# A Hymba-style layer on one core: the scheduler's simulated-timeline mode, and the down-weight sums moved beside the last short convolutions and the o heads

## The chip, the core and the metric

The kernel runs on one core of one Trainium2 chip. The metric is the device time of one execution in microseconds (us). Five engines take part, each with its own instruction stream that it executes in order: TensorE (PE, with its weight loads shown apart as PEld), VectorE (DVE), ScalarE (ACT), GpSimd (POOL) and SyncE (SP). All transfers between HBM and the on-chip memory are issued from SP's stream, so their issue is in order too: a transfer whose buffer is not free holds up every transfer behind it. An engine that waits for a semaphore holds up its own stream in the same way.

## What is computed

The reference is one layer on 2176 tokens of width 1024: 128 context tokens and 2048 latent tokens that read them. Cut to what matters:

```python
shift1, scale1, gate1, shift2, scale2, gate2 = jnp.split(mod, 6, axis=-1)
h = rmsnorm(x, norm1) * (1 + scale1) + shift1
z = h @ w_in                       # short-conv inputs, q, k, v, o, gates
y_sc = sc_b * conv3(sc_c * sc_x)   # short convolution
h_m = mlstm_bidir(q, k, v, gates, C0, n0, m0)   # forward and backward scans, 4 heads, chunks of 128
x = x + gate1 * (concat([y_sc, norm(h_m) * sigmoid(o)]) @ w_out)
h2 = rmsnorm(x, norm2) * (1 + scale2) + shift2
up = conv3(h2 @ w_up)              # 2 x 2816 columns, conv over a 64-wide grid
x = x + gate2 * ((silu(gg) * a) @ w_down)
```

`mod` comes from the conditioning vectors: `silu(c) @ w_mod + b_mod`, a vector of 6 x 1024 for each of two kinds of tokens. The outputs are the new x and the final context states of the scans.

## The kernel before

**Tiles.** The 2176 tokens lie in six blocks (`BL`): five of 384 columns and one of 256. `BA` are the blocks 0 to 2, `BB` the blocks 3 to 5. Every product in float32 is made from three matmuls of a rounded high part and a low rest: weight high by input high, weight high by input low, weight low by input high (`gemm`, L206 to L208; for v and gates L352 to L354, with the tokens as the stationary operand). `load_w` (L110 to L115) loads a weight slab into `wst` (2 buffers), ACT makes its high part `wh` (L112), POOL its low part `wl` (L115).

**Stages, in order of time.** (1) The modulation vectors of the first norm: 16 loads of 512 KB of `w_mod` (`mod_pe`, L485, tile `wm` with 5 buffers) with 8 PE matmuls each (L488); DVE adds the bias (L490), and the input blocks are normalised (`apply`, L178 to L188: `xt`, `hH`, `hL`). (2) v and gates of block 3, 4, 5 (`vg`), then k heads, q heads and short convolutions of these blocks (`heads`, `shortconv`, results stored in `kD`, `qD`, `yD`). (3) o heads of the same blocks, weight by weight of a block (`by_block`), while h of the blocks 0 to 2 is made (`make_h`, with loads `xt<-in_x` L148, and PE's column transposes L140). (4) v and gates of blocks 0 to 2. (5) The gate phase (`gate_phase`, L640 on, with transposes on PE at L665), woven with the k heads of blocks 0 to 2. (6) The scans (`Mix`, L834 to L881), woven with the rest of the heads and short convolutions of blocks 0 to 2. (7) The output projection (`w_out`, L426 to L470, results stored in `xD`), with the second norm's statistics (L129, L132, L133, L237, L239) and the sums that a Strassen-like scheme needs of the normed input (`sums`, L244 to L265: `F<-xD` loads, DVE sums, stores to `tD`). (8) The up projection (`w_up`, loads `st` L287, parts L295/L296, products L1045 to L1047): two halves of the tokens (`hf`), 22 rows of weight tiles `j` in each, seven products `i` in each row. The seven inputs ("slots") of a half are loaded from `tD` (L275) and split by ACT (L280, `tH`) and DVE (L281, `tL`); the convolution over the grid follows on ACT and DVE (L988 to L1010), and `sums(1)`, the sums for the second half, goes beside the first rows. (9) The down projection (`w_down`, L1199 to L1201), again with seven products, of sums of the weights.

**The sums of the down weights.** `down_sums` (L558 to L584) makes those last sums ahead of time. It works in 8 steps of a load of four pieces of 352 KB (`xs<-in_w_down`, L566), four DVE sums (L576 to L580) and four stores (`wsD<-xs`, L583). `pin` (`tc.keep_in_program_order`) keeps the loads and the DVE sums in the order of the source. The tile `xs` has four buffers and lies in the pool `start`, whose memory the pool `gt` of the gate phase takes over.

**What sets the order.** The source is a set of generators: `run(g, side, every)` takes a step of `g` and then one of `side`. The order written down in this way is a priority, not the order of execution: the tile framework's scheduler orders the instructions of each engine afterwards, subject to data dependencies, buffer counts and `pin`. In the program before it does that in its default mode (`tile.TileContext(nc)`, L1296).

Of the kernel before, what the change touches and what calls it, by code (L numbers as in the profile page):

```python
# [12 lines left out]
AF = mybir.ActivationFunctionType  # L13
# [25 lines left out]
BA = (0, 1, 2)  # L39
BB = (3, 4, 5)  # L40
# [17 lines left out]
def hymba_kernel(ctx: ExitStack, tc: tile.TileContext, I, O):  # L58
# [42 lines left out]
    def run(g, side=None, every=1):  # L101
        for i, _ in enumerate(g):
            if side and i % every == 0:
                next(side, None)
# [90 lines left out]
    def make_h(b, src, norm):  # L195
        return apply(b, load_x(b, src, xp, "xt", 2), norm)
# [120 lines left out]
    with ExitStack() as ph1:  # L317
# [52 lines left out]
        def heads(blocks, hs, w0, dst, func, scale, by_block=False):  # L370
            if by_block:
                ws = [load_w(I["w_in"][w0 + h]) for h in range(H)]
                for b in blocks:
                    for h in range(H):
                        head(ws[h], b, h, hs, dst, func, scale)
                        yield
                return
            for h in range(H):
                w = load_w(I["w_in"][w0 + h])
                for b in blocks:  # L380
                    head(w, b, h, hs, dst, func, scale)
                    yield
# [99 lines left out]
        with tc.tile_pool(name="start", bufs=1, side="right") as stp:  # L482
# [41 lines left out]
            def mod_dve():  # L524
                for mt in range(16, 48):
                    st = stp.tile([P, 1024], F32, name="wm", bufs=5)
                    Q.dma_start(st, I["w_modr"][mt - 16])
                    t = stp.tile([P, 2], F32, name="mt", bufs=2)
                    for v in range(2):
                        jk = pm.tile([P, 2, 512], F32, name="y")  # L530
                        V.scalar_tensor_tensor(jk.rearrange("p a b -> p (a b)"), st, 1.0, cB[:, v], op0=ALU.mult, op1=ALU.mult,
                                               accum_out=t[:, v:v + 1])
                    V.tensor_scalar(modT[:, mt, :], t, bmod[:, mt:mt + 1], None, op0=ALU.add)
                    if mt == 39:
                        affine(1, 0, KT)
                    yield
# [10 lines left out]
            def first_stats():  # L547
                for b in BA:
                    ss = squares(b, load_x(b, I["x"], xp, "xt", 2))
                    yield  # L550
                    inv_rms(ss, BL[b][1], rcol(b))
                    yield
# [31 lines left out]
                    t = nt  # L584

            late()
            side = chain(first_stats(), mod_dve())
            run(vg((3,), hs, ws), prep(4))
            run(vg((4,), hs, ws), prep(5))
            run(vg((5,), hs, ws))  # L590
            run(heads(BB, hs, 16, kD, AF.Copy, 1.0), side, 2)
            run(heads(BB, hs, 12, qD, AF.Copy, QS), side, 2)
            run(shortconv(BB, hs), side)
            run(side)
            go = heads(BB, hs, 20, oD, AF.Sigmoid, 1.0, by_block=True)
            dsums = down_sums()
            for b in BA:
                run(islice(go, 4), dsums)
                hs[b] = make_h(b, I["x"], 0)
            run(vg(BA, hs, load_vg(0) + load_vg(1)), dsums)  # L600
            run(dsums)

        ml = phr.enter_context(tc.tile_pool(name="ml", bufs=1, side="right"))

# [296 lines left out]
                    next(fill, None)  # L901


        with tc.tile_pool(name="gt", bufs=1, side="right") as gt:
            gph = gate_phase()
            kh = heads(BA, hs, 16, kD, AF.Copy, 1.0)
            while True:
                try:
                    next(gph)
                except StopIteration as e:  # L910
                    cols, colc, decB = e.value
                    break
                next(kh, None)
                next(kh, None)
            run(kh)
# [392 lines left out]
```

## Time and profile before

| | |
|---|---|
| Median of 3 runs | 2552.67 us (2550.52 to 2553.85) |
| The profiled execution's own time | 2555.34 us |
| Its span in the trace | 2553.5 us |
| PE busy | 2470.7 us of the span, 16127 matmuls |
| DVE, ACT, POOL busy | 1649.2, 1112.7, 566.4 us |
| Bytes moved | 444.60 MB, mean 174 GB/s |

So 1.84 us lie around the span, and the profiled execution is 2.67 us above the median of the runs. Busy time of PE includes the time in which its granted clock is low, so a stage can be short of work and show few idle microseconds: the rows by stage show busy time and granted clock (PEclk, 1.00 is full speed) side by side, then the DMA share and the GB/s moved. A chain-of-waits row is a start, a duration and the work or transfer that the following step waited for.

### The profile page before, as it was taken

The page shows a single profiled execution, that of the slowest core. Times are in us where ns is not written, and L with a number is a line of the kernel's source. Part 1 is how long each engine was busy: PE and PEld are TensorE (multiplying, and loading weights), DVE is VectorE, ACT ScalarE, POOL GpSimd, SP SyncE. Part 2 cuts the span into 40 slices and gives each one's busy share as a digit, 9 for nine tenths or more (in the row PEclk, how much of TensorE's full clock was granted, in tenths as well). Part 3 has the DMA queues.
Part 4 walks back from the last instruction along what each step waited for, and adds up shares of the span by engine and source line. Part 5 has one row for each costly group of instructions (what it writes and reads, how often), then busy time and mean ns, then how long its engine had stood idle before and what let it go on. Part 6 is the DMA issues. An engine that isn't in the chain of part 4 may idle for free.

```text
span 2553.5 us, 42533 instructions
## 1 busy us (share of the span) xinstructions
PE 2470.7 (97%) x16127; PEld 2366.4 (93%) x16127; DVE 1649.2 (65%) x2741; ACT 1112.7 (44%) x2035; POOL 566.4 (22%) x470
## 2 busy tenths in 40 slices
PE   8999998999999889899999999899999999999998
PEld 8999997999999889899999999788888899999998
DVE  3993255222356666678678666877776796687586
ACT  4522142222245554455455444555554554444342
POOL 2442142211233443422112111122122100000000
PEclk9999998999999999999999999999999999999999
DMA  7771188356567887775125222522222277767674
GB/s 280 252 270 69 66 278 284 117 168 178 180 191 241 253 261 226 251 270 173 67 81 181 83 83 82 171 92 99 83 91 93 72 227 227 242 214 225 187 218 135
DMA packets 281423, 444.60 MB, mean 174 GB/s; under 512 B 23282, under 2 KB 206722, under 8 KB 279554
## 3 DMA queue, kind: packets, MB, share of 16 engines
q1 hardware_dynamic: 281218, 441.88, 53.0%
q8 instruction: 127, 2.08, 0.3%
q14 instruction: 78, 0.64, 0.1%
HBM read 335.31 MB, written 106.48 MB: 173 GB/s over the span
## 4 chain that ended last, share of the span: by engine, by line
PE 77%; DMA 8%; DVE 7%; issue 3%; ACT 3%; POOL 2%; SPq 1%; DVEq 0%; ACTq 0%; POOLq 0%
PE acc L206 8%; PE acc L208 8%; PE acc L207 8%; PE pa L1045 7%; PE pa L1047 7%; PE pa L1046 6%; PE d L1200 5%; PE d L1201 5%; PE d L1199 5%; PE pb L1045 3%; PE pb L1046 3%; PE pb L1047 3%; PE pc L1045 2%; PE pc L1046 2%; PE pc L1047 2%
## 5 line engine op out<-in xcount | busy, mean ns | idle before, releaser
L206 PE MATMUL acc<-hH,wh 128*128 128x384 f32 (+1 forms) x1536 | 515.4, 336 | 8.2 <-DVE row L462 5.5
L208 PE MATMUL acc<-hH,wl 128*128 128x384 f32 (+1 forms) x1536 | 508.0, 331 | 0.5 <-POOL wl L115 0.5
L207 PE MATMUL acc<-hL,wh 128*128 128x384 f32 (+1 forms) x1536 | 507.8, 331 | 0.0
L1199 PE MATMUL d<-bh,wh 128*128 128x272 f32 x1232 | 355.7, 289 | 0.7 <-ACT raw L1057 0.7
L1201 PE MATMUL d<-bh,wl 128*128 128x272 f32 x1232 | 356.1, 289 | 0.0
L1200 PE MATMUL d<-bl,wh 128*128 128x272 f32 x1232 | 355.4, 289 | 0.0
L1045 PE MATMUL pa<-tH,wh 128*128 128x288 f32 (+1 forms) x1056 | 347.7, 329 | 3.7 <-DVE raw L1059 2.0
L1047 PE MATMUL pa<-tH,wl 128*128 128x288 f32 (+1 forms) x1056 | 346.9, 329 | 1.0 <-DVE wl L296 1.0
L1046 PE MATMUL pa<-tL,wh 128*128 128x288 f32 (+1 forms) x1056 | 346.9, 329 | 0.0
L296 POOL TENSOR_TENSOR wl<-st,wh 128x512 fp32r<-128x512 f32 x132 | 184.2, 1396 | 696.2 <-ACT wh L295 668.4
L115 POOL TENSOR_TENSOR wl<-wst,wh 128x512 fp32r<-128x512 f32 (+1 forms) x160 | 235.2, 1491 | 441.8 <-ACT wh L112 417.5
L206 PEld LDWEIGHTS acc<-hH,wh 128*128 128x128 f32 x1536 | 292.9, 191 | 10.2 <-DVE row L462 5.1
L208 PEld LDWEIGHTS acc<-hH,wl 128*128 128x128 f32 x1536 | 292.6, 190 | 1.2 <-POOL wl L115 1.0
L207 PEld LDWEIGHTS acc<-hL,wh 128*128 128x128 f32 x1536 | 293.1, 191 | 0.3 <-issue 0.2
L988 DVE SCALAR_TENSOR_TENSOR tt<-raw,fw,tt 128x127 f32<-128x127 f32 (+4 forms) x264 | 246.1, 953 | 2.7 <-ACT tt L994 1.5
L1199 PEld LDWEIGHTS d<-bh,wh 128*128 128x128 f32 x1232 | 231.9, 188 | 1.3 <-ACT raw L1057 1.1
L1200 PEld LDWEIGHTS d<-bl,wh 128*128 128x128 f32 x1232 | 231.9, 188 | 0.2
L1201 PEld LDWEIGHTS d<-bh,wl 128*128 128x128 f32 x1232 | 231.8, 188 | 0.0
L1045 PEld LDWEIGHTS pa<-tH,wh 128*128 128x128 f32 x1056 | 198.4, 188 | 20.2 <-ACT c L1052 2.2
L1047 PEld LDWEIGHTS pa<-tH,wl 128*128 128x128 f32 x1056 | 199.1, 189 | 17.0 <-DVE wl L296 1.4
L1046 PEld LDWEIGHTS pa<-tL,wh 128*128 128x128 f32 x1056 | 198.7, 188 | 15.7
L295 ACT ACTIVATE wh<-s 128x512 fp32r<-128x512 f32 x176 | 110.9, 630 | 177.7 <-PE pc L1046 92.0
(239 smaller groups left out, 4848.6 us busy)
## 6 DMA issues: line engine op xcount, KB each, us to landing
st<-in_w_up SPq DMA_DIRECT2D x88, 512.0 KB, 4.3
us<-uD SPq DMA_DIRECT2D x48, 544.0 KB, 5.0
wst<-in_w_in SPq DMA_DIRECT2D x48, 512.0 KB, 4.0
uD<-tt SPq DMA_DIRECT2D x44, 544.0 KB, 2.7
R<-nD SPq DMA_DIRECT2D x34, 512.0 KB, 4.2
wm<-in_w_modr SPq DMA_DIRECT2D x32, 512.0 KB, 5.2
wst<-in_w_out SPq DMA_DIRECT2D x24, 512.0 KB, 4.7
st<-wsD SPq DMA_DIRECT2D x32, 384.0 KB, 3.3
```

The source lines that it names most:

```text
L115: G.tensor_sub(wl[:, a:a + n // 2], st[:, a:a + n // 2], wh[:, a:a + n // 2].bitcast(F32))
L206: PE.matmul(acc[:, :n], w_h, hH[:, k, :n], start=(k == 0), stop=False)
L207: PE.matmul(acc[:, :n], w_h, hL[:, k, :n], start=False, stop=False)
L208: PE.matmul(acc[:, :n], w_l, hH[:, k, :n], start=False, stop=(k == KT - 1))
L296: (G if on_pool else V).tensor_sub(wl, a, wh.bitcast(F32))
L988: V.scalar_tensor_tensor(o, i, w, o, op0=ALU.mult, op1=ALU.add)
L1045: PE.matmul(acc, wh[:, w], rh, start=(kk == 0 and i in (0, 1, 5)), stop=False, skip_group_check=True)
L1046: PE.matmul(acc, wh[:, w], rl, start=False, stop=False, skip_group_check=True)
L1047: PE.matmul(acc, wl[:, w], rh, start=False, stop=(kk == 3), skip_group_check=True)
L1199: PE.matmul(acc, wh[:, c], uh, start=(kk == 0), stop=False)
L1200: PE.matmul(acc, wh[:, c], ul, start=False, stop=False)
L1201: PE.matmul(acc, wl[:, c], uh, start=False, stop=(kk == KH - 1))
```

## The change

Three edits. First, the scheduler is asked for its mode `schedule_with_timeline_sim=True`, in which it orders the instructions against another simulated timeline; every instruction of the program may take another place on its engine. Second, `down_sums()` is appended to `side`, which is taken along in the k heads, q heads and short convolutions of the blocks 3 to 5 and now in the o heads too; what is left of it is run after the o heads. Third, `vg(BA, ...)` is taken out of the pool `start` and run without side work, just before the pool `gt`.

```diff
@@ -584,21 +584,18 @@
             late()
-            side = chain(first_stats(), mod_dve())
+            side = chain(first_stats(), mod_dve(), down_sums())
             run(vg((3,), hs, ws), prep(4))
             run(vg((4,), hs, ws), prep(5))
             run(vg((5,), hs, ws))
             run(heads(BB, hs, 16, kD, AF.Copy, 1.0), side, 2)
             run(heads(BB, hs, 12, qD, AF.Copy, QS), side, 2)
             run(shortconv(BB, hs), side)
+            go = heads(BB, hs, 20, oD, AF.Sigmoid, 1.0, by_block=True)
+            for b in BA:
+                run(islice(go, 4), side)
+                hs[b] = make_h(b, I["x"], 0)
             run(side)
-            go = heads(BB, hs, 20, oD, AF.Sigmoid, 1.0, by_block=True)
-            dsums = down_sums()
-            for b in BA:
-                run(islice(go, 4), dsums)
-                hs[b] = make_h(b, I["x"], 0)
-            run(vg(BA, hs, load_vg(0) + load_vg(1)), dsums)
-            run(dsums)
@@ -901,6 +898,7 @@
+        run(vg(BA, hs, load_vg(0) + load_vg(1)))
         with tc.tile_pool(name="gt", bufs=1, side="right") as gt:
@@ -1293,7 +1291,7 @@
-    with tile.TileContext(nc) as tc:
+    with tile.TileContext(nc, schedule_with_timeline_sim=True) as tc:
```

Line numbers up to 584 stay; those of the gate phase and the scans fall by 3 (L665 becomes L662), those behind L899 by 2 (L1045 becomes L1043).

How the instructions move is seen at three places. The **first** is SP's stream between the o heads and the gate phase. `vD<-rv` stores v of a chunk, `wsD<-xs` a sum of down weights, `wst<-in_w_in` loads the first k weights of the gate phase. Before:

```order
L566 DMA xs<-in_w_down 128x704 x4
L358 DMA vD<-rv 128x258
L583 DMA wsD<-xs 128x704 x4
L358 DMA vD<-rv 128x258 x3
L583 DMA wsD<-xs 128x704 x4
L358 DMA vD<-rv 128x258 x4
L110 DMA wst<-in_w_in 128x1024
L668 DMA sm_4511<-in_state_m 1x8
```

Now:

```order
L566 DMA xs<-in_w_down 128x704 x2
L148 DMA xt<-in_x 128x4x384
L110 DMA wst<-in_w_vg 128x1056
L358 DMA vD<-rv 128x258
L110 DMA wst<-in_w_in 128x1024
L358 DMA vD<-rv 128x258 x2
L583 DMA wsD<-xs 128x704 x2
L110 DMA wst<-in_w_in 128x1024
L583 DMA wsD<-xs 128x704
L358 DMA vD<-rv 128x258
L583 DMA wsD<-xs 128x704
L358 DMA vD<-rv 128x258 x3
```

Before, the last sums are stored behind 14 of the 18 stores of v of the blocks 0 to 2, and the first k weights are loaded behind all of them; now the last sum is stored behind four of them, and both loads of k weights stand ahead of that store. The first load of down weights moves too: from behind the last short convolution's last store (`yD<-yr`) to behind that of the last but one. On PE the first transposes of the gate phase (`S`, from `fc` and `ic`) stood between the last v product and the first k product. Before:

```order
L354 MATMUL acc_4388<-wh_3817,hL_3765 128x264
L665 MATMUL S_4505<-ident_78,fc_4426 128x128
L665 MATMUL S_4508<-ident_78,ic_4425 128x128
L206 MATMUL acc_4447<-hH_3396,wh_4442 128x384
L207 MATMUL acc_4447<-hL_3397,wh_4442 128x384
```

Now the products of two k heads' blocks (`acc_4447` and `acc_4475`, 24 matmuls each) stand ahead of the first transpose, and the third's ahead of the second:

```order
L206 MATMUL acc_4475<-hH_3642,wh_4442 128x384
L207 MATMUL acc_4475<-hL_3643,wh_4442 128x384
L208 MATMUL acc_4475<-hH_3642,wl_4444 128x384
L662 MATMUL S_4505<-ident_78,fc_4426 128x128
L206 MATMUL acc_4527<-hH_3808,wh_4442 128x384
```

The **second** place is SP's stream at the start, from the third load of `w_mod` on (`wm<-in_w_mod`; `cB` are the conditioning vectors of both kinds, `xs` and `xt` input blocks). Before, up to the last of the 16:

```order
L485 DMA wm<-in_w_mod 128x1024 x2
L148 DMA xt<-in_x 128x4x384 x2
L485 DMA wm<-in_w_mod 128x1024 x4
L110 DMA wst<-in_w_vg 128x1056 x2
L485 DMA wm<-in_w_mod 128x1024 x8
```

Now, from the eighth of them on, up to the last and the first load behind it:

```order
L485 DMA wm<-in_w_mod 128x1024
L148 DMA xs<-in_x 128x4x256 x2
L485 DMA wm<-in_w_mod 128x1024 x2
L110 DMA wst<-in_w_vg 128x1056
L485 DMA wm<-in_w_mod 128x1024
L110 DMA wst<-in_w_vg 128x1056
L485 DMA wm<-in_w_mod 128x1024 x2
L148 DMA xt<-in_x 128x4x384
L485 DMA wm<-in_w_mod 128x1024 x2
L110 DMA wst<-in_w_in 128x1024
L485 DMA wm<-in_w_mod 128x1024
L527 DMA wm<-in_w_modr 128x1024
```

The inputs of block 5 (`xs`), the second pair of `w_vg` slabs, one input piece of block 0 (`xt`) and one k weight have moved ahead of the last loads of `w_mod`; in the rows just above these the 1 MB of `cB`, the masks and convolution weights and the inputs of block 4 (two loads of 768 KB) have moved ahead of the eighth.

The **third** place is SP's stream where the up projection begins. `F<-tD_72` loads a slot of the first half, `xD<-row` stores the output projection, `tD_73<-F` stores sums for the second half, `eD` and `uD` are stores of the first rows. Before:

```order
L464 DMA xD<-row 128x384
L275 DMA F<-tD_72 128x1152
L464 DMA xD<-row 128x256
L287 DMA st<-in_w_up 128x1024
L439 DMA row<-in_x 128x384
```

Now:

```order
L464 DMA xD<-row 128x256
L275 DMA F<-tD_72 128x1152
L275 DMA F<-tD_72 128x2304 x4
L999 DMA eD<-raw_11462 128x128
L287 DMA st<-in_w_up 128x1024
L275 DMA F<-tD_72 128x2304
L287 DMA st<-in_w_up 128x1024
L999 DMA eD<-raw_11463 128x128
L244 DMA F<-xD 128x2x256 x4
L265 DMA tD_73<-F 128x7x256 x2
L1008 DMA uD<-tt 128x1088
```

Before, five stores of `xD` stand behind the first slot's load, and the next two slots' loads stand between them; now all slots' loads stand behind the last store of `xD`. The stores of `tD_73` have moved forward as well: before, four of the eight stand at this place and the other four behind the weights of six further rows `j`; now all eight stand here, the last behind the weights of three further rows.

## The prediction

> **What bounds the kernel now.** I read the page first, then busy time and granted clock by stretch, then the waits of PE and the chain of waits in the stretches that fall short. The page:
>
> ```profile
> PE 2470.7 (97%) x16127; PEld 2366.4 (93%) x16127; DVE 1649.2 (65%) x2741; ACT 1112.7 (44%) x2035; POOL 566.4 (22%) x470
> ...
> PE 77%; DMA 8%; DVE 7%; issue 3%; ACT 3%; POOL 2%; SPq 1%; DVEq 0%; ACTq 0%; POOLq 0%
> ```
>
> PE is the bound: it is busy in all but 82.8 us of the span (2553.5 less 2470.7), and the change neither adds nor takes away a matmul, a transfer or a sum. So all that it can win or lose is time in which PE waits or runs at a low clock, and the question is at which places the new order lets it wait. Where PE is steady there is nothing to win; the first fence below shows stretches at full clock beside the one place where the old order was worst, the gate phase (columns: stretch and its length, PE busy with matmuls, PEld, DVE, ACT, POOL, granted clock, DMA share, GB/s):
>
> ```profile
> 320.00:384.00 64.00, 61.59 (x426) 61.20 (x424) 37.20 (x60) 29.53 (x62) 28.39 (x25) 1.00 0.81 281
> 384.00:400.00 16.00, 10.19 (x65) 9.92 (x66) 12.96 (x19) 6.03 (x12) 7.77 (x9) 0.79 0.79 272
> 400.00:432.00 32.00, 32.00 (x267) 32.00 (x266) 12.22 (x23) 3.98 (x12) 0.89 (x9) 1.00 0.92 318
> 432.00:448.00 16.00, 10.17 (x43) 8.86 (x42) 8.63 (x30) 6.00 (x9) 5.42 (x6) 0.68 0.70 228
> 448.00:512.00 64.00, 63.24 (x348) 60.60 (x348) 16.68 (x52) 18.24 (x37) 15.19 (x12) 0.95 0.34 115
> ```
>
> PE has two holes of 5.8 us each, and the clock falls with them. Its waits there (engine, tile, line, what it waited for, us in all, times, longest) and the chain of waits:
>
> ```profile
> PE acc L352 <- ACT xt L186: 5.2, 1, 5.2
> PE S L665 <- DVE fc L658: 4.9, 1, 4.9
> PE acc L353 <- POOL rv L356: 1.6, 1, 1.6
> PE st L140 <- DVE xt L178: 1.4, 1, 1.4
> ```
>
> ```profile
> 399.61 7.05 DMA wsD<-xs
> ...
> 410.94 7.74 DMA wsD<-xs
> ...
> 422.00 8.12 DMA wsD<-xs
> 430.19 5.38 DMA wsD<-xs
> ...
> 439.33 0.49 PE S L665
> ```
>
> The stores of the down weights' sums lead from 399.6 to 435.6, and the gate phase, whose tiles take over the memory of `xs`, can begin only behind the last of them. The transposes and the first k weights, which stand behind all stores of v in SP's stream, come late for that reason. The other hole, at 384 to 400, is the making of h of block 0, on DVE behind the sums.
>
> **Part 1, the sums and the gate phase.** In the new order the first load of down weights stands one short convolution earlier, the last store behind four instead of fourteen stores of v, and the first k weights ahead of it; the gate transposes stand behind two and three finished k products. So the 5.2 and the 4.9 should go: 10.1 us. The clock that the holes cost is, by the rows, 0.21 of 10.19, 0.32 of 10.17 and 0.05 of 63.24: 2.1 + 3.3 + 3.2 = 8.6 us. Together 18.7. The 1.6 and the 1.4 are chains on ACT, DVE and POOL that no row of the new order shortens for certain; I leave them in. Term: -18, with bounds of -23 (idle 2.4 + 5.8 + 5.8 + 0.8 = 14.8, and 8.6) and -8 (the waits go only in part, below).
>
> [...]
>
> **Part 2, the start.** The sixteenth load of `w_mod` gates the last slice (k = 7) of h of block 3 and with it the end of every v product.
>
> ```profile
> 0.00:10.00 10.00, 4.30 (x20) 4.33 (x21) 0.56 (x4) 1.50 (x2) 0.40 (x8) 1.00 0.70 246
> 10.00:20.00 10.00, 8.99 (x78) 8.83 (x78) 4.52 (x11) 3.96 (x8) 0.00 (x0) 1.00 1.04 404
> 20.00:30.00 10.00, 8.34 (x76) 8.26 (x75) 4.30 (x15) 4.49 (x7) 6.10 (x6) 1.00 0.80 316
> 30.00:40.00 10.00, 10.00 (x92) 10.00 (x92) 6.31 (x17) 3.83 (x7) 3.20 (x3) 1.00 0.85 278
> 48.00:56.00 8.00, 8.00 (x56) 8.00 (x55) 1.38 (x5) 3.89 (x8) 0.10 (x1) 0.79 0.89 282
> ```
>
> ```profile
> PE acc L354 <- POOL hL L188: 2.7, 1, 2.7
> ```
>
> ```profile
> 51.44 0.22 PE acc L352
> ```
>
> Before, 16 loads of 0.52 MB, two slabs of 0.54 and two input pieces of 0.79, with the small ones 11.2 MB, stand up to and with it. At the mean of the first four rows (311 GB/s) that is 36 us. Now two more slabs, `cB` (1.05), four `xs` (2.6), one `xt`, one k weight and the masks stand ahead of it: 17.5 MB, 56 us at 311 GB/s and 43 at the 404 of the second row, so 7 to 20 us later. Against that, PE has more v products ahead of the first that needs k = 7 (53 matmuls against 23): 30 of them at half of the 0.22 of the chain's row (its stretch has the clock 0.79) are 3.3 us, and the wait of 2.7 us for POOL, which was splitting slabs, is covered. So +1 to +14; in the middle +7, of which I take off 1, since the loads pulled ahead needn't be waited for later. Term: +6, bounds 0 and +14. [...]
>
> **Part 3, scans and output projection.** The largest wait is one inside the scans:
>
> ```profile
> PE y L851 <- DVE R L838: 14.9, 7, 4.4
> ```
>
> PE's order is nearly the old one there; the weights of the output projection and the input rows are loaded earlier, some matmuls follow their DVE inputs more closely. I take -3, bounds -8 (half of the 14.9 goes) and +5 (a third more of it).
>
> **Part 4, where the up projection begins.**
>
> ```profile
> 1060.00:1090.00 30.00, 24.55 (x147) 24.02 (x146) 23.49 (x42) 14.39 (x28) 10.70 (x9) 0.87 0.89 288
> 1090.00:1120.00 30.00, 29.15 (x193) 28.88 (x192) 21.61 (x36) 12.37 (x20) 5.57 (x5) 0.96 0.83 274
> 1120.00:1150.00 30.00, 27.54 (x194) 26.97 (x193) 21.80 (x27) 19.18 (x31) 6.92 (x5) 0.94 0.72 256
> 1150.00:1200.00 50.00, 49.54 (x372) 49.33 (x371) 48.44 (x74) 29.09 (x50) 12.97 (x10) 1.00 0.54 176
> 1200.00:1400.00 200.00, 200.00 (x1503) 199.79 (x1501) 144.49 (x226) 98.97 (x171) 41.30 (x31) 1.00 0.34 116
> ```
>
> ```profile
> PE acc L206 <- DVE row L462: 4.1, 2, 3.3
> PE st L129 <- DVE rc L132: 2.8, 1, 2.8
> PE pc L1045 <- ACT tH L280: 2.5, 2, 2.2
> PE st L237 <- ACT rb L239: 2.2, 1, 2.2
> ```
>
> ```profile
> 1128.85 8.30 DMA F<-tD
> ...
> 1138.24 1.16 ACT tH L280
> ```
>
> ```profile
> L250 DVE SCALAR_TENSOR_TENSOR F<-F,ab,rb 128x512 f32<-128x512 f32 x16 | 12.6, 804 | 0.9 <-DMA F<-xD 0.9
> ...
> L257 DVE TENSOR_TENSOR F<-F 128x256 f32<-128x256 f32 x8 | 8.6, 1069 | 0.0
> ...
> L255 DVE TENSOR_TENSOR F<-F 128x256 f32<-128x256 f32 x8 | 6.9, 859 | 0.1
> L254 DVE TENSOR_TENSOR F<-F 128x256 f32<-128x256 f32 x8 | 6.0, 744 | 1.3 <-ACT F L252 1.3
> ```
>
> Before, this place costs 11.6 us of waits and 0.13 of 24.55, 0.04 of 29.15 and 0.06 of 27.54, 6.0 us, of clock: 17.6. In the new order all slots' loads stand behind the last store of `xD`. A slot takes 8.3 us of load, 1.2 on ACT and, as I take it, as much on DVE: 10.7, with two buffers 5.4 each, while a product of 24 matmuls lasts 24 x 200 / 1503 = 3.2: five slots, 2.2 us late each, 11 us. The eight steps of the sums for the second half cost DVE 34.1 us (12.6 + 8.6 + 6.9 + 6.0). Half of them move forward, 17 us, into the 80 us of the third and fourth row, in which DVE has 8.2 + 1.6 = 9.8 free: 7 us too much. With the same 6 for the clock the place costs 24 to 25. Term: +7; bounds 0 (the old waits fall away as the new ones come) and +24 (the rival below).
>
> **Part 5, the rest.** In the steady rows of the up projection's second half two matmuls of one product stand ahead of the one before; the row of 200.00 us busy in 200 covers it in the first half: 0, at most +4 if the weight split falls behind. In the down projection the chain of the final norm stands somewhat further from its use, and its waits are these:
>
> ```profile
> PE st L140 <- POOL fr L133: 2.3, 3, 1.1
> ```
>
> Term: -2, bounds -3 and +2.
>
> **Sum.** -18 + 6 - 3 + 7 - 2 = -10 us on the profiled execution's 2555.34 (span 2553.5 and 1.84 around it): 2545.3. That execution lies 2.67 above the median of the runs, so I forecast 2552.67 - 10 = 2542.7 as the median.
>
> **Rivals.** *The losses stay hidden:* the two loading orders cost nothing, since transfers run at the 404 GB/s of the start and the slots' loads find the queue empty; then -20 at the gates, 0 at the start, -4 and -2 behind: -26, 2526.7. For it speaks the DMA share of 0.34 from 1200 on; against it 0.72 to 0.89 just before.
>
> *The wait moves (no difference):* the third and fourth slab of `w_vg` for blocks 0 to 2 now stand among the last sums. The sums move 64 pieces of 0.36 MB, 23 MB, 82 us at the 281 GB/s of 320 to 384, and with 9 MB of slabs and inputs 114. The 21 products of the last short convolution and the o heads last some 21 x 24 x 0.15 = 76 us (64 us for 426 matmuls is 0.15 each). So the v products could meet their third slab late by some 10 us, the gain at the gates falls to 8, and the sum is 0: 2552. That the mode leaves the order elsewhere as it was, so that only the -18 acts, is ruled out by the rows of the order at the start.
>
> *Slower, the up projection's begin:* DVE executes in order, and if the moved sums stand ahead of the slots' low parts and of the adds that free PSUM, all of the 17 us come on PE's path, not 7, and the first slot's load (8.3) is bare. The place then costs 17 + 11 + 8.3 + 6 = 42, +24 against 17.6 before; the sum is +7: 2559.7. It decides from a loss of about 22 there on, and for it speaks the row with DVE at 48.44 of 50; against it, that row had PE at 49.54.
>
> **How the numbers follow.** What a measurement of this kernel can tell from no change is about 0.2%, 5.1 us. Forecast 0.42, hidden losses 0.18, moved wait 0.20, slower 0.20. The forecast's own spread (some -18 to -3) gives 0.34 to faster and 0.08 to no difference; the moved wait gives 0.17 to no difference and 0.03 to slower. Faster 0.18 + 0.34 = 0.52, no difference 0.25, slower 0.20 + 0.03 = 0.23. The range reaches from the hidden losses with the gates at their bound (-30) to a little past the slower rival (+11): 2523 to 2564; the likeliest case's own is 2535 to 2550.
>
> **What would show it.** Right: in the changed profile the waits at L352 and at the gate transposes (L662) under 1 us each, clock 1.00 from about 380 to 500, no `wsD` stores in the chain of waits there; a PE wait for `w_mod` or `hL` between 40 and 65 longer than before; busy PE under 140 in the 150 us where the up projection begins. Wrong: v products of blocks 0 to 2 that wait for weight slabs (the moved wait), no longer wait at the start, DVE over 95% for 100 us with PE waiting behind it (the slower rival), or a new hole in the scans, which I priced at almost nothing.

## The result, and the profile after

The changed kernel takes 2564.41 us (median of 5 runs, 2563.72 to 2567.97), the kernel before 2552.67 us (median of 5, 2550.52 to 2558.14). The ratio is 1.0052, 95% interval [1.0037, 1.0068]: slower by 0.5%, where 2542.7 was forecast. The profiled execution took 2563.72 us (span 2561.9), 8.4 more than before's; the medians are 11.7 apart, since before's profiled execution lay 2.7 above its median and this one 0.7 below its own. The page after:

```profile
PE 2475.9 (97%) x16127; PEld 2367.0 (92%) x16127; DVE 1648.6 (64%) x2741; ACT 1111.2 (43%) x2035; POOL 564.4 (22%) x470
...
PE 81%; DMA 7%; DVE 6%; issue 2%; ACT 2%; POOL 1%; SPq 1%; DVEq 0%; POOLq 0%; ACTq 0%
```

The engines run as many instructions as before, and PE is busy 5.2 us longer for the same matmuls. Busy time and clock hide in each other (in the changed kernel PE is busy for 3.93 of the 4 us from 400 on, at a clock of 0.50), so for each stage I work out one number, the **lag**: each matmul of the trace is counted at the time that its shape takes in a steady stretch (0.174 us with 384 columns, 0.133 with 288, 0.126 with 272, and so on, 2392.9 us in all in every kernel here), and the lag is the elapsed time less the work that PE has begun by then. It holds idle time, low clock and everything else that PE loses. The stretches end where PE has done 56, 464, 957, 1100, 1900 and 1970 us of work, so that they hold the same amount in every kernel; in the kernel before that is at 75, 512, 1060, 1220, 2038 and 2109 us. Lag gained in each stretch, in us; the last column is the sum, which is the span less 2392.9:

| kernel | start | gates | scans | up begin | up, rest | down begin | end | sum |
|---|---|---|---|---|---|---|---|---|
| before | 19.3 | 28.8 | 54.7 | 17.6 | 17.6 | 1.4 | 21.2 | 160.6 |
| after | 24.4 | 13.6 | 55.6 | 28.1 | 17.5 | 9.5 | 20.3 | 169.0 |
| after less before | +5.1 | -15.2 | +0.9 | +10.5 | -0.1 | +8.1 | -0.9 | +8.4 |

Three places speak in the trace. **The gates** of the changed kernel, by stretch (columns as in the prediction):

```profile
384.00:400.00 16.00, 9.31 (x72) 8.79 (x70) 9.47 (x18) 7.70 (x15) 4.90 (x5) 0.92 0.83 310
400.00:432.00 32.00, 31.93 (x248) 31.93 (x249) 6.87 (x24) 6.26 (x13) 8.76 (x20) 0.93 0.47 143
432.00:448.00 16.00, 16.00 (x110) 15.97 (x109) 4.95 (x12) 7.35 (x11) 7.37 (x6) 1.00 0.56 174
448.00:512.00 64.00, 64.00 (x370) 60.97 (x369) 19.71 (x65) 18.08 (x38) 12.96 (x10) 1.00 0.30 94
```

and all of PE's waits of the stretch from 75 to 512 us:

```profile
PE acc L352 <- ACT wh L112: 5.1, 1, 5.1
PE acc L353 <- POOL wl L115: 1.6, 1, 1.6
```

The second hole, at 432 to 448, is gone and its clock is full; the first stands where it stood. The wait is now put down to the high part of a `w_vg` slab, but ACT makes that part directly behind its work on an input block, and the loads of both stand one behind the other in SP's stream (issued at 386.06 and 386.55), behind the sums' stores and loads. So the trace does not part the slab from the input block. The chain:

```profile
382.64 1.90 DVE xs L580
384.70 0.19 SPq L583
...
386.06 8.38 DMA xt<-in_x
...
395.77 0.61 ACT xt L186
396.39 0.98 ACT wh L112
```

The 0.92 and 0.93 of the rows are means: in finer rows PE has half its clock, and then all of it at once. The trace's clock records have it at half from 397.4 to 404.2.

```profile
400.00:404.00 4.00, 3.93 (x18) 3.94 (x19) 3.96 (x4) 0.00 (x0) 4.00 (x6) 0.50 0.48 144
404.00:432.00 28.00, 28.00 (x232) 28.00 (x232) 2.90 (x20) 6.26 (x13) 4.76 (x15) 1.00 0.47 143
```

**The up projection's begin**, the 160 us from 1060 to 1220, before and after:

```profile
1060.00:1220.00 160.00, 150.77 (x1050) 149.21 (x1049) 128.70 (x200) 84.94 (x143) 40.36 (x31) 0.96 0.67 223
```

```profile
1060.00:1220.00 160.00, 144.74 (x982) 139.51 (x981) 128.86 (x205) 84.31 (x142) 44.16 (x32) 0.96 0.67 222
```

PE does 68 matmuls fewer in the same time, 9.0 us at the 0.133 of the prediction's steady row. DVE is busy for as long; what it does differs. Two of PE's waits after, and two pieces of the chain of waits:

```profile
PE st L129 <- DVE ss L470: 2.8, 1, 2.8
PE pa L1045 <- DVE wl L296: 2.5, 1, 2.5
```

```profile
1097.76 0.89 DVE F L250
...
1103.09 0.37 DVE tL L262
1103.45 0.48 DVE ss L470
1104.07 1.41 PE st L129 x6
...
1145.05 0.74 DVE F L250
...
1146.13 3.19 DVE tt L986 x4
1149.32 0.61 DVE wl L296
1149.98 0.40 PE pa L1045
```

Both times longer work stands in DVE's row ahead of the short instruction for which PE waits, but it is not the same work. Ahead of the last statistics `ss` stand pieces of `sums(0)` (only these have the `tL` of L262), which the up projection itself needs next. Ahead of the weight's low part `wl` stand a piece of `sums(1)`, which is for the second half, and four of the convolution. The 16 instructions with which its steps begin (L250) all stand between 1140 and 1204 now; before, eight of them stood there and the other eight came only from 1334 on. The view of L250 for 1130 to 1220, before and after:

```profile
L250 DVE SCALAR_TENSOR_TENSOR F<-F,ab,rb x8: 737/739/751, 1146.2 to 1186.6; 128x512 f32<-128x512 f32 x8
```

```profile
L250 DVE SCALAR_TENSOR_TENSOR F<-F,ab,rb x16: 736/744/1784, 1140.0 to 1204.4; 128x512 f32<-128x512 f32 x16
```

**The down projection's begin**, before and after:

```profile
2040.00:2110.00 70.00, 69.31 (x478) 65.18 (x477) 63.58 (x62) 41.03 (x57) 3.43 (x2) 1.00 0.71 224
```

```profile
2040.00:2110.00 70.00, 63.82 (x409) 57.71 (x408) 60.02 (x60) 39.61 (x53) 3.54 (x2) 0.98 0.63 196
```

Where PE was busy in 69.3 of 70 us there is now a chain of waits through DVE (`bl` L1124 are low parts of inputs, `cur` L1116 the sums of inputs for later products, `tt` the convolution's last rows):

```profile
2085.22 1.00 DVE bl L1124
2086.22 1.15 DVE cur L1116
2087.37 1.27 DVE tt L1007
2088.65 5.81 DMA uD<-tt
2094.54 0.41 ACT top L1202
2094.99 0.39 PE d L1197
```

```profile
PE d L1197 <- ACT top L1202: 2.7, 1, 2.7
```

The splits and sums for the next products of the down projection now run while the up projection still needs DVE. By this chain the copy `top`, which frees an accumulator, waits until the convolution's last store (`uD<-tt`) has landed, and that convolution stood on DVE behind `bl` and `cur`. (The view of waits puts ACT's 2.3 us ahead of `top` down to a sum of L1116, which ended at the same time as that store; the trace does not part the two.)

On DVE, four instructions for later (L1096 at 2048.8 and 2052.6, L1124 at 2050.2 and 2051.4) have their place ahead of the up projection's last weight part on that engine (L296 at 2054.6); before, it was one (a `bl`, 1.3 us). The up projection's last convolution ends at 2088.6, 34 us behind that weight part, and before it took 21.5 (2049.0 to 2070.6).

### The profile page after: what moved, and what is told of

The parts are those of the page before. It is cut to its first block, busy times and chain, and to the rows that moved or that the text cites. A ratio compares the mean times of both kernels' runs of the same rounds, so it can differ in the third digit from the quotient of the medians.

```text
span 2561.9 us, 42510 instructions
## 1 busy us (share of the span) xinstructions
PE 2475.9 (97%) x16127; PEld 2367.0 (92%) x16127; DVE 1648.6 (64%) x2741; ACT 1111.2 (43%) x2035; POOL 564.4 (22%) x470
## 4 chain that ended last, share of the span: by engine, by line
PE 81%; DMA 7%; DVE 6%; issue 2%; ACT 2%; POOL 1%; SPq 1%; DVEq 0%; POOLq 0%; ACTq 0%
PE acc L206 8%; PE acc L208 8%; PE acc L207 8%; PE pa L1045 6%; PE pa L1043 6%; PE pa L1044 6%; PE d L1197 6%; PE d L1199 6%; PE d L1198 6%; PE pb L1045 3%; PE pb L1043 3%; PE pb L1044 3%; PE pc L1045 2%; PE pc L1043 2%; PE pc L1044 2%
## 5 line engine op out<-in xcount | busy, mean ns | idle before, releaser
L1043 PE MATMUL pa<-tH,wh 128*128 128x288 f32 (+1 forms) x1056 | 348.5, 330 | 3.9 <-ACT wh L295 1.7
L1045 PE MATMUL pa<-tH,wl 128*128 128x288 f32 (+1 forms) x1056 | 343.7, 330 | 5.1 <-DVE wl L296 4.9
L296 POOL TENSOR_TENSOR wl<-st,wh 128x512 fp32r<-128x512 f32 x132 | 179.9, 1365 | 727.2 <-ACT wh L295 681.6
L1045 PEld LDWEIGHTS pa<-tH,wl 128*128 128x128 f32 x1056 | 199.5, 189 | 22.0 <-DVE wl L296 6.0
L1043 PEld LDWEIGHTS pa<-tH,wh 128*128 128x128 f32 x1056 | 199.4, 189 | 21.7 <-ACT wh L295 2.4
L1043 PE MATMUL pb<-tH,wh 128*128 128x288 f32 (+1 forms) x528 | 174.4, 331 | 3.9 <-ACT wh L295 3.3
```

Source lines behind the costliest of these rows:

```text
L296: (G if on_pool else V).tensor_sub(wl, a, wh.bitcast(F32))
L1043: PE.matmul(acc, wh[:, w], rh, start=(kk == 0 and i in (0, 1, 5)), stop=False, skip_group_check=True)
L1045: PE.matmul(acc, wl[:, w], rh, start=False, stop=(kk == 3), skip_group_check=True)
```

## The experiments

The theory after this reading: the mode orders the engines anew, which clears the holes at the gates, and at three places puts work for later (loads at the start, `sums(1)` at the up projection's begin, input splits at the down projection's begin) ahead of what PE needs next; the edit of the source is worth little by itself. Rivals: the gain at the gates comes from the edit of the source and only the loss from the mode; or the losses have other causes, and pulling that work back moves the wait to the next instruction. Lag gained per stretch in the runs that follow (in us, the stretches as above), with their ratios to the kernel before:

| kernel | start | gates | scans | up begin | up, rest | down begin | ratio, interval |
|---|---|---|---|---|---|---|---|
| src_only | 19.6 | 26.5 | 54.7 | 11.3 | 15.6 | 1.4 | 1.0004 [0.9993, 1.0016] |
| mode_only | 24.9 | 10.4 | 55.5 | 30.8 | 16.8 | 9.0 | 1.0043 [1.0028, 1.0058] |
| u_pin | 23.9 | 13.1 | 56.8 | 24.7 | 13.6 | 9.0 | 1.0027 [1.0016, 1.0038] |
| stat_pin | 25.8 | 12.2 | 60.9 | 21.9 | 17.7 | 7.1 | 1.0036 [1.0024, 1.0049] |
| d_pin | 23.9 | 14.1 | 57.8 | 29.9 | 18.0 | 6.3 | 1.0056 [1.0044, 1.0068] |
| start_pin | 44.6 | 33.1 | 62.8 | 28.9 | 13.7 | 8.6 | 1.0188 [1.0167, 1.0208] |
| start_behind | 21.1 | 14.8 | 56.5 | 29.1 | 13.8 | 6.8 | 1.0042 [1.0028, 1.0057] |
| mode_fix | 25.4 | 12.9 | 55.2 | 17.4 | 13.6 | 3.6 | 0.9993 [0.9983, 1.0003] |
| src_early | 17.6 | 17.3 | 56.4 | 11.3 | 15.7 | 1.4 | 0.9966 [0.9953, 0.9978] |
| src_swap | 20.5 | 19.1 | 56.1 | 14.1 | 16.6 | 1.4 | 0.9971 [0.9959, 0.9982] |
| src_q1 | 18.9 | 11.3 | 58.5 | 14.4 | 15.3 | 1.4 | 0.9935 [0.9918, 0.9951] |

A lag is of one execution, and executions of one kernel differ by some us (before: 2540.6 to 2558.14 over all chips), so a lag says where, and the ratio decides how much. The profiled execution of mode_fix lies 5.8 below its median, that of start_pin 11.7 above; those of the other nine lie within 2.9.

**The two halves of the change.** The source of the changed kernel in the default mode, and the source of before in the new mode:

```diff
-    with tile.TileContext(nc, schedule_with_timeline_sim=True) as tc:
+    with tile.TileContext(nc) as tc:
```

> The new source in the scheduler's default mode. Theory (the source edits bring the gain at the gate phase, the mode brings the losses at the start, at the up projection's begin and at the down projection's begin): the hole of some 16 us at the gate phase is gone and nothing else moves, so 2537 us, 15 to 16 below the kernel before. Rival (the mode, which puts two k products ahead of the gate transposes, brings the gain too): within 4 us of the kernel before, 2549 to 2556.

```diff
-    with tile.TileContext(nc) as tc:
+    with tile.TileContext(nc, schedule_with_timeline_sim=True) as tc:
```

> The old source in the mode with the simulated timeline. Theory (source brings the gain, mode the losses): the losses without the gain, 2564 + 16 = 2580 us, at least 2572. Rival (the mode brings gain and losses alike): 2560 to 2568, as the changed kernel.

The mode alone is 2562.55 us, the source alone 2549.24. All of what the changed kernel shows stands in the row of mode_only: start 24.9, gates 10.4, up begin 30.8, down begin 9.0. The source alone wins nothing that can be measured. Its wait at the gates and the chain there:

```profile
PE acc L352 <- ACT wh L112: 13.9, 1, 13.9
```

```profile
378.69 0.67 SPq L583
379.40 0.73 SPq L110
380.17 9.80 DMA wst<-in_w_vg
```

Both old holes have become one of 13.9 us: the load of the `w_vg` slab stands in SP's stream behind the sums' last stores (L583). That is the moved wait of the prediction's second rival, in the default mode. So the gates' gain in the changed kernel is the mode's.

How the mode gets it is not what the theory of these runs said. In mode_only the last sums are stored even later than before, but the first k weights (L110) are loaded ahead of them and not behind them, and PE has k products to do until the first transpose comes at 450.4. SP's stream before, and in mode_only:

```profile
427.66 2.85 SPq L583 DMA_DIRECT2D wsD<-xs  x4
...
435.37 0.42 SPq L110 DMA_DIRECT2D wst<-in_w_in  x1
```

```profile
387.97 1.43 SPq L110 DMA_DIRECT2D wst<-in_w_in  x1
...
436.46 0.88 SPq L583 DMA_DIRECT2D wsD<-xs  x2
```

**The up projection's begin, in two parts.** First, in the changed kernel, one sum of each step of `sums(1)` on DVE keeps the place of the source:

```diff
+                        if hf and k >= 4 and i0 == 0:
+                            pin(ins)
```

> The changed kernel, with the first DVE instruction of each step of the sums for the second half tied behind the DVE instruction that stands before it in the source, so that the steps spread over sixteen rows of the up projection. Theory (these steps crowd DVE, and PE waits for weight parts and splits behind them): the waits of PE between 1140 and 1220 go, some 8 to 10 us: 2555 us. Rival (the slots' loads behind the last stores of the output projection are the cause): within 3 us of the changed kernel's 2564.

2556.41 us; up begin 28.1 to 24.7, and 3.9 less in the stretch behind it, in which the second half of the tokens begins. By the ratio the two are only just apart: its interval ends at 1.0038, and that of the changed kernel begins at 1.0037. Second, the last statistics' matmuls (L129) and those of `sums(1)` (L237) keep their place on PE:

```diff
+                    if hf:
+                        pin(mm)
...
-                        defer.append(lambda: stats(grp, sss))
+                        defer.append(lambda: stats(grp, sss, pin))
```

> The changed kernel, with the column sums of the last statistics and the spreads for the second half's sums tied on PE behind the matmul that stands before them in the source, so that they stand behind three products of the up projection instead of one and none. Theory (PE waits there in order for the last statistic, 2.8 us, and then runs at a low clock): 6 to 9 us less than the changed kernel, a ratio to the kernel before of about 1.002. Rival (DVE is late at this place with everything, so that the next product waits just as long): within 3 us of the changed kernel, a ratio of 1.004 to 1.006.

2558.45 us; up begin 28.1 to 21.9, but the scans' stretch has 5.3 more, and by the ratio the run can't be told from the changed kernel. Nor does it test PE's row alone: with these ties the scheduler also put `sums(1)` on DVE back to where it was before, 8 of the 16 instructions of L250 (L252 here) between 1154 and 1180 and the rest from 1334 on. So both ties spread `sums(1)`, and both lower the lag here; what PE's own order adds is not shown.

**The down projection's begin.** The input splits on ACT and one sum on DVE for the next products keep the place of the source:

```diff
+            if (g, i) == (0, 1):
+                pin(ins)
...
-            S.activation(bh, x, AF.Copy)
+            at(S.activation(bh, x, AF.Copy))
```

> The changed kernel, with the look-ahead work of the down projection's first product (the splits of the second product's inputs on ACT and their differences on DVE) tied behind what stands before it in the source. Theory (this work stands ahead of the last rows' convolution and of the copies that free PSUM, and PE waits for those, 6 us and clock): 6 to 8 us less than the changed kernel, a ratio of 1.0025. Rival (the weight loads of the down projection that stand earlier on SP are the cause): no change, 1.004 to 1.006.

No gain: 2564.97 us, as the rival forecast. In its profile PE's wait for `top` is gone and waits of 1.0 and 0.9 us stay; the lag is 6.3 where it was 9.5. The ties changed nothing of what they were for on DVE: the same four instructions stand ahead of the last weight part (L296, now at 2058.9).

**The start, twice.** First all loads that the mode had pulled ahead were put back into the source's order (masks, `fw`, `cB`, two `w_vg` slabs, the `xs` inputs):

```diff
-            Q.dma_start(x[:, :, :n], src[4 * kh:4 * kh + 4, :, t0:t0 + n].rearrange("k p t -> p k t"))
+            at(Q.dma_start(x[:, :, :n], src[4 * kh:4 * kh + 4, :, t0:t0 + n].rearrange("k p t -> p k t")))
...
-            ws += load_vg(1)
+            ws += load_vg(1, pin)
```

> The changed kernel, with the loads of the masks, the convolution weights, cB, the second pair of w_vg slabs and the inputs of blocks 4 and 5 each tied behind the transfer that stands before it in the source. Some 13 MB instead of 17.5 stand up to the last load of w_mod. Theory (bytes ahead of that load cost the time at the start): 5 to 6 us less than the changed kernel, 2559. Rival (one input load of block 0, which stays ahead of the last three loads of w_mod and waits for the slice k = 3, holds them up): within 2 us of 2564.

This says nothing of the cause: 2594.7 us. The pinned inputs of blocks 4 and 5 came behind loads and stores that the mode had left ahead of them, and PE waited 19.9 us in two waits for statistics of input blocks (`ss`, L166).

Then the same loads were tied directly behind the last load of `w_mod` instead, with `behind`:

```diff
-            ws += load_vg(1)
+            ws += load_vg(1, behind)
```

> The changed kernel, with all loads that had moved ahead of the last of w_mod (second pair of w_vg slabs, masks, convolution weights, cB, inputs of blocks 4, 5 and 0) tied behind that one load and behind nothing else: the bytes up to it are those of the kernel before, 11.2 MB. Theory (bytes ahead of that load cost 5 to 6 us at the start): the first 100 us of PE's work end 5 us earlier than in the changed kernel, a ratio of 1.003. Rival (what the start wins is paid by the inputs of block 4 that come later): PE's work up to 100 us ends when it did, a ratio of 1.005.

2558.45 us; the start 24.4 to 21.1. The direction is the predicted one and the size is 3.3 of the 5.1 lost, but the rival has a part in it: up to 82 us PE's waits for `w_mod` fall from 12.6 to 9.1, while those behind the input blocks grow from 1.9 to 5.5, and the sum stays the same. By the ratio it can't be told from the changed kernel either.

**All ties together.** u_pin, stat_pin and start_behind, the splits of d_pin, and now also the low parts `bl` (all but the first of a product) behind the up projection's last weight part on DVE (the expectation calls them weight splits; they are splits of inputs):

```diff
+            if tie and c:
+                tc.add_manual_dep(ins.ins, tie[-1].ins.name,
+                                  mybir.DependencyInfo(mybir.DependencyClass.NoSync, mybir.DependencyReason.DATA),
+                                  reason="behind the last weight part")
```

> The changed kernel with the three places tied at once: the loads that had moved ahead at the start stand directly behind the last w_mod load; the first sums(1) sum of each step on DVE, the last statistics (L129) and sums(1)'s own matmuls (L237) on PE keep the place of the source; and in the down projection the weight splits for later products stay behind the last weight part of the current one. Theory (the mode's new order gains about 16 us at the gates, 7 in the scans, and gives 5 back at the start, 19 at the up projection's begin and 8 at the down projection's): what the ties won one by one (2.8 at the start, 5.4 and 6.6 at the up projection's begin, 3.1 at the down projection's) adds up nearly, since they lie at different places: span 12 to 18 us below the changed kernel's 2561.9, that is 2544 to 2550, ratio to before 0.997 to 1.000. Rival (the waits only move: behind the tied instruction stands another that comes as late, as DVE is full at the up projection's begin whichever goes first): the ties overlap or cost elsewhere, span above 2555, ratio 1.002 or more.

2548.83 us, 0.9993 where the changed kernel has 1.0052: the ties win 0.59%, 15 us (20.7 between the two profiled executions), and leave the gates' gain as it is. (The expectation counts a loss of 19 at the up projection's begin and a gain of 7 in the scans; by the lag it is a loss of 10.5 and one of 0.9.) The row of mode_fix for the up projection's begin:

```profile
1060.00:1220.00 160.00, 148.67 (x1061) 145.20 (x1060) 121.63 (x189) 83.36 (x143) 38.89 (x27) 0.99 0.54 182
```

79 matmuls more than in the changed kernel. The up begin's lag falls by 10.7 (3.4 and 6.2 one by one), that behind it by 3.9, the down begin's by 5.9 of the 8.1 lost (3.2 with d_pin): on DVE one `bl` stands ahead of the last weight part again, though the two weight parts of the down projection (L1096 in the changed kernel) still do. How much of that is DVE's row, and how much ACT's, these runs do not part. The early loads of down weights, d_pin's rival, were tied in no run; four of them stand ahead of the last `uD` store but one here too, as in the changed kernel (before, two), so by these lags they make up no more than the 2.2 us by which 3.6 is above the 1.4 of the kernel before. The waits that remained at the up begin are others, so the rival of the moved wait holds for a part: 3.9 us for slots' parts (`tH`) and 3.1 for the output projection's last `row`.

At the start the tie won nothing this time (25.4): the last load of `w_mod` is issued at 35.1 and not at 42.9, but the inputs of blocks 4 and 5 are loaded at 39 to 45 us and not at 19 to 22, and the loss has moved from the stretch of 20 to 40 us to that of 60 to 80, where PE waits 5.2 us behind their statistics and normalising. The changed kernel:

```profile
20.00:40.00 20.00, 14.04 (x80) 13.20 (x81) 11.50 (x27) 13.09 (x25) 8.25 (x8) 0.74 1.04 393
...
60.00:80.00 20.00, 18.96 (x159) 18.88 (x158) 20.00 (x43) 11.50 (x27) 7.34 (x12) 1.00 0.64 205
```

mode_fix:

```profile
20.00:40.00 20.00, 18.17 (x148) 18.20 (x149) 8.57 (x22) 4.97 (x9) 7.74 (x8) 0.91 0.81 271
...
60.00:80.00 20.00, 14.80 (x95) 14.22 (x94) 20.00 (x39) 10.25 (x23) 8.36 (x12) 0.74 0.73 260
```

**The gates without the mode.** The mode brought the k weights ahead of the last stores. The other way is to have the sums done earlier, and the default mode can do that too. Three versions of the side work, all in the default mode with the new source. A step behind every product in the k and q heads, not every second:

```diff
-            run(heads(BB, hs, 16, kD, AF.Copy, 1.0), side, 2)
-            run(heads(BB, hs, 12, qD, AF.Copy, QS), side, 2)
+            run(heads(BB, hs, 16, kD, AF.Copy, 1.0), side)
+            run(heads(BB, hs, 12, qD, AF.Copy, QS), side)
```

> The new source in the default mode, with a step of the side work at every product of the k and q heads and not at every second one, so that the sums of the down weights begin some twelve products earlier and all of them are stored ahead of the first v weights of blocks 0 to 2. Theory (the hole at the gate phase is the time by which the sums' transfers end too late, and 13.9 us of it only moved to the v weights in the new source alone): the hole goes, 14 to 16 us below the kernel before, a ratio of 0.994. Rival (the transfers then collide with the second norm's modulation weights and the inputs, and the wait moves on): ratio 0.998 to 1.002.

2541.41 us. The gates' hole is gone, and a new wait of 4.7 us between 100 and 160 us takes part of the gain, for statistics (L129) behind the modulation's products on DVE (`modT`, L533).

The sums ahead of the modulation's products, every second step as before:

```diff
-            side = chain(first_stats(), mod_dve(), down_sums())
+            side = chain(first_stats(), down_sums(), mod_dve())
```

> The scheduler's default mode with the new source, and the side work in another order: the sums of the down weights directly behind the first statistics, so beside the q heads and short convolutions, and the rest of the modulation's products behind them. All slabs of w_vg for the blocks 0 to 2 are then loaded behind the last sum, on a queue that is empty by then. Theory (the gate phase's hole is a matter of when the last sum is stored, and the source alone missed the gain only because its sums ended beside the v products; the mode isn't needed): no wait over 2 us for a slab, transposes without a wait, clock 1.00 there; the gate stage gains 16 to 20 us, and the 7 us that the earlier sums in the k heads lost at the start aren't lost here, as the first statistics stay first. Span 2534 to 2540, ratio 0.993 to 0.996. Rival (any order of side work that empties the gate phase puts its load on another place, as every version so far but one did): the modulation's loads, now beside the o heads, come in the way of the input blocks there, a new hole of 8 us or more by the o heads, ratio 0.998 or more.

2542.8 us: again without the hole, and again with a new wait. It is for what the rival named, the loads of the modulation (`w_modr`), but beside the short convolutions and not by the o heads; their DVE step `cr` stands behind the products (L531) that wait for such a load. The wait and the chain there:

```profile
PE acc L206 <- DVE cr L394: 5.2, 3, 4.1
```

```profile
200.87 8.17 DMA wm<-in_w_modr
...
215.93 0.41 DVE cr L394
```

And the denser side work in the q heads alone:

```diff
-            run(heads(BB, hs, 12, qD, AF.Copy, QS), side, 2)
+            run(heads(BB, hs, 12, qD, AF.Copy, QS), side)
```

> The scheduler's default mode with the new source; the side work takes a step behind every product in the q heads (before, and in the changed kernel, behind every second), and stays behind every second in the k heads. So the sums end earlier than with the source alone, and the first statistics, whose late place cost 7 us where the k heads too were filled, keep theirs. Theory (the gate phase's hole is only a matter of when the last sum is stored and the v slabs loaded; the denser side work hides where DVE has room): the stage up to 384 us loses 4 us or less, the gate stage has no wait over 2 us and gains 16 us, behind it as with both heads filled: span 2531 to 2540, ratio 0.993 to 0.996. Rival (the denser side work in the q heads and short convolutions costs what it won, as with the sums ahead of the modulation, which lost 11.8 us there while its adds queued on DVE ahead of the products' results): waits for `cr` or `yr` of 4 us and more between 150 and 300 us, span above 2541, ratio 0.997 or more.

2534.81 us (2529.88 to 2538.56), ratio 0.9935 [0.9918, 0.9951]: the fastest of all, 16 us below the kernel before on the same chip. (The expectation puts the loss of src_swap down to the sums' adds; the chain above shows the modulation's products.) Its last sum is stored at 369 us, before at 430. PE is busy through the gates (under the 0.95 lies a stretch of half clock: the chain has the v products 0.22 us apart from 385.17 to 390.23, as the changed kernel has them at half clock, against 0.12 at full), the begins of the up and the down projection are as in the default order, and the scans' stretch has 3.8 more lag than before:

```profile
384.00:448.00 64.00, 63.42 (x455) 62.67 (x456) 11.51 (x44) 16.09 (x29) 16.56 (x26) 0.95 0.34 107
```

## Why the prediction was wrong

The sum was -10 and the profiled executions show +8.4, 18.4 apart. By its steps:

- **Part 5, the step that failed.** "In the down projection the chain of the final norm stands somewhat further from its use ... Term: -2, bounds -3 and +2." The stretches behind the up projection's begin gave +7.1 together, all of it from the begin of the down projection (+8.1), far outside the bounds: 9.1 of the 18.4. I had priced the final norm alone; the begin of the down projection, where PE was busy 69.3 of 70 us, is not in the sum at all. As far as the ties show, it was free of waits because the old order kept most splits for later products behind the up projection's last weight part; mode_fix, with that order put back in part, has 3.6 us of lag there, and d_pin, whose ties left DVE's row as it was, 6.3.
- **Part 4, near in size, half of the mechanism wrong.** +7 forecast, +10.5 measured, within the bounds. The 11 us for late slots did not come: the six slots' loads are issued from 1105.5 to 1130.1, before from 1105.6 to 1133.1, and PE's waits for `tH` are 2.4 us, before 2.5. That the size is near is luck to that extent. The other half, which is also the third rival's mechanism, holds: `sums(1)` moved forward on DVE, all of it and not half, and spreading it takes lag away; in the chain it delays a weight's part rather than the slots' parts, and it does not cost 24. Also, the base was high: five profiles of the default order (before, src_only, src_early, src_swap, src_q1) have a lag of 11.3 to 17.6 at this place, before's the highest, while the five of the new mode without a tie there (after, mode_only, d_pin, start_behind, start_pin) have 28.1 to 30.8.
- **Part 1, near in size, half of the cause wrong.** -18 forecast, -15.2 measured. The forecast waits at the transposes (L662) are gone, but the wait at L352 did not fall below 1 us: 5.1 are left, at a slab and an input block. The forecast names two reasons together: the sums' earlier place, and k weights and k products ahead of what the gate phase waits for. src_only begins its sums earlier and gains next to nothing (26.5); mode_only has the k weights ahead, stores its last sums later than before and gains it all (28.8 to 10.4). So the second rival, with its slabs among the last sums, was half right: it is the whole story in the default mode (13.9 us), and at most 5.1 us of it in the new one. The clock's price was misread too: the 0.95 over 64 us (3.2 of the 8.6) is not what the second hole left behind. The clock was full again by 448, and fell to half at 492, towards the end of PE's small transposes (`y`, L731, 12 of them that begin between 489.5 and 492.4):

```profile
448.00:464.00 16.00, 16.00 (x93) 15.47 (x93) 1.74 (x9) 4.89 (x7) 7.58 (x6) 1.00 0.62 210
...
492.00:499.00 7.00, 7.00 (x24) 6.98 (x25) 1.47 (x3) 0.11 (x1) 0.00 (x0) 0.52 0.56 171
```

That loss is gone as well in the changed kernel (1.00 from 432 on), for a reason that the prediction did not have.
- **Part 2, right in size.** +6 forecast, +5.1 measured, and the wait is the forecast one; that the bytes ahead of the last load are the price is not shown, since PE waits for the inputs instead where they are tied behind it. The waits for `w_mod` went from 6.7 to this:

```profile
PE acc L488 <- DMA wm<-in_w_mod: 12.6, 6, 5.8
```

- **Part 3.** -3 forecast, +0.9 measured, within the bounds.

The other half of the error is thus 2.8 at the gates, 3.9 at the scans and 3.5 at the up begin, less 0.9 at the start. The slower rival's time, 2559.7, was the nearest to the result, but its single mechanism made up only a part of the loss; what I did not weigh is that an order that is new everywhere can lose at several places at once, each a few us. How much of the loss at the start can be had back by any order of the loads stays open, and so does why stat_pin has 5.3 us more in the scans' stretch.

## What to carry to other kernels

A change of the scheduler's mode is a change at every place of the program, so price the places that are without a wait now by what covers them, and look in the new order for work for later ahead of the last urgent instruction at every change of stage; the steady stretches did not care (17.6 and 17.5 us of lag in the rest of the up projection). Test the halves of such a change apart: here the mode won 13 to 18 us at one place (against src_only and against before) and lost more at three others, and the source edit, which looked like the cause of the gain, won nothing alone. Once the place was understood (the stores of the sums and the urgent loads behind them in SP's one stream, where PE waited 13.9 us for such a load in src_only), there were two ways out: the loads ahead of the stores, as the mode has them, or the stores done earlier. The second took one number more on top of the source edit, in the default order, and made the whole kernel 0.65% faster; whether the old source with sums as early does as well was not run. And look at finer rows before putting a price on a low mean clock: it can be a short stretch of half clock, and not where the wait was (here 0.95 from 448 to 512, with 1.00 up to 464 and 0.52 in the 7 us from 492 on).

## What the runs showed of the hardware

At the start the transfers ran faster than I had reckoned with, and PE was short of them nevertheless. The changed kernel, by stretch:

```profile
10.00:20.00 10.00, 8.59 (x68) 8.24 (x67) 4.84 (x13) 5.42 (x10) 0.40 (x1) 1.00 1.05 378
...
30.00:40.00 10.00, 7.54 (x40) 7.24 (x41) 7.55 (x17) 7.97 (x18) 1.61 (x2) 0.66 1.05 396
```

378 and 396 GB/s in these two stretches of 10 us, where the prediction's mean was 311; in the second PE waited 5.6 us for `w_mod`, and its clock was 0.66.

In the changed kernel PE waited 5.1 us at the gates, from 392.3 to 397.4. The clock records have half the clock from 397.4 to 404.2, 6.8 us, and the full clock from there to 885.5; in the 6.8 us PE waited another 1.6 and was busy for 5.2, which at half clock is 2.6 us of lost work beside the waits. It is not the price of a clock that stays a little low: the rows with 0.92 and 0.93 each hold a part of that one stretch.
